# Delta net values and keys put into token order once per head, by VectorE in 32x32 blocks and a trip through DRAM

## The chip, the cores and the metric

The kernel runs on one core of one Trainium2 chip. The metric is the device time of one launch in microseconds (us), lower is better; the median of several launches is given where there are several. TensorE (PE) multiplies matrices, VectorE (DVE), ScalarE (ACT) and GpSimd (POOL) work on tiles, SyncE (SP) mostly starts transfers (DMAs). Each engine takes its instructions strictly in its own order and waits on semaphores for the others.

## The reference

Two layers on a sequence of 1024 tokens of width 1024. Layer 0 has retention (4 heads of 128) and a gated delta net (4 heads of 128), then a feed-forward net; layer 1 has an RG-LRU and a second feed-forward net. The change is in the delta net of layer 0, whose chunkwise form reads:

```python
lmat = where(strict, einsum('bhnid,bhnjd->bhnij', k_beta, kc) * decay, 0)
u, w = triangular_solve(lmat + eye, [vc * bc, k_beta * exp(gc)])
def step(s, (u_n, w_n, a_n, qd_n, kt_n, cd_n)):
    v_new = u_n - w_n @ s
    o = qd_n @ s + a_n @ v_new
    s = s * cd_n + kt_n.T @ v_new
```

with `qkv = silu(causal_dwconv(...))`, `k_tail = kc * exp(g_last - gc)` and `vc` the values by chunk. The kernel takes chunks of 128 tokens, so there are 8 chunks.

## The kernel before

Activations lie as channels x tokens (a head is a tile of 128 channels by 1024 tokens). All large products run as three float32r passes, L313, L314 and L315 in `mm3`: high weights by high data, high by low, low by high. One such instruction of 512 columns is called a *main matmul* below. A projection of 128 output channels (a *unit*) is 48 main matmuls: 8 blocks of the input, 3 passes, and two halves of the tokens. Its weights come in two *quarters*; each is loaded to a `raw` tile (L257, SP), split by ACT into `whi` (L267) and by DVE into `wlo` (L268), in rings of 7 and 6 buffers. The first main matmul of a quarter needs `whi`, the third needs `wlo`.

The program calls `slot()` after each three main matmuls, which steps generators (`lanes`) that carry the small work: the delta net's gates, the substitution, `merge`, `scans` and retention. The tile framework's scheduler then orders the instructions of each engine by its own model of durations; the order is fixed when the program is built, and the chip follows it.

The part of `_mix0` that matters, in order of the units on PE:

- `subst`: 31 steps on DVE invert all 32x32 diagonal blocks of L in tiles `lb` (slots 14 and 15), `tb` (16 and 17) and `tt` (18 and 19); the inverse goes to `t_dram` twice, straight and turned (L1337, L1339).
- `gates2((0, 1))`: units 12 and 13; evacuation by L373, tanh on ACT (L1167), product on DVE (L1168), then a store to `g_dram` (L1716).
- `merge(h, i)` for four heads, i the half of the tokens: blocks come back from `t_dram` (L1353, one set on SP, the turned one on POOL), ACT copies them (L1363, L1364), and PE and ACT take turns: L1369, then L1372 on ACT, L1378 and L1382, then L1385 and L1386 on ACT, L1392, then L1394, L1398. The two halves of a head run together.
- the loop over the value heads: units 24 to 27 (`conv_head`: L373, L1264, three L1266, L1268, L1269), each then stored to `v_dram`.
- `gates2((2,))`: unit 14, a gate like 12 and 13.
- ACT's queue loads the two rotary tables into the halo tiles (L1735, L1736) and DVE multiplies them by the row scale (L1737, L1738).
- `rot_head`: units 0, 4, 1, 5, 2, 6, 3, 7 for retention, evacuated by L1538, L1540 and L1541 on DVE and an addition on POOL.
- `scans`, beside the rotary units: per chunk, `scan_load` brings `v` and `q` from DRAM, `scan_inside` turns the values (L1461, four transposes on PE), scales them (L1462), forms the scores (L1465), turns the keys (L1473) and scales them (L1474, for all chunks but the last); `scan_state` carries the state (L1485, L1491, L1498, L1508, L1509).

Of the kernel before, what the change touches and what calls it, by code (L numbers as in the profile page):

```python
# [13 lines left out]
F32 = mybir.dt.float32  # L14
F32R = mybir.dt.float32r
AF = mybir.ActivationFunctionType
ALU = mybir.AluOpType
AX = mybir.AxisListType

P = 128  # L20
# [3 lines left out]
HALF = 512  # L24
NCH = T // P
NH = 4
# [67 lines left out]
def bc_mid(ap, n):  # L94

    return ap.unsqueeze(1).to_broadcast([ap.shape[0], n, ap.shape[1]])


def bc_last(ap, n):

    return ap.unsqueeze(2).to_broadcast([ap.shape[0], ap.shape[1], n])


class Block:
# [57 lines left out]
    def col(self, name, i):  # L162
        off, n = COLS[name]
        assert i < n
        return self.cols[:, off + i:off + i + 1]
# [978 lines left out]
    def mix0(self, gain):  # L1144
        tc = self.tc
        self.q_dram = tc.dram_tile([NCH, P, HALF], F32, name="q_dram")
        self.ry_dram = tc.dram_tile([4, NCH, P, P], F32, name="ry_dram")
        self.v_dram = tc.dram_tile([NCH, P, HALF], F32, name="v_dram")
        self.gc_dram = tc.dram_tile([NH, NCH, P], F32, name="gc_dram")
        self.l_dram = tc.dram_tile([P, 32, 32], F32, name="l_dram")  # L1150
        self.t_dram = tc.dram_tile([2, P, 32, 32], F32, name="t_dram")
        self.y_dram = tc.dram_tile([8, P, T], F32, name="y_dram")
        self.rv_dram = tc.dram_tile([NCH, P, HALF], F32, name="rv_dram")
        self.g_dram = tc.dram_tile([NH, P, T], F32, name="g_dram")
        self.X = [[(self.slots1(4 * k + n), self.slots1(4 * k + 2 + n)) for n in range(2)] for k in range(KT)]
        with tc.tile_pool(name="l0", bufs=1) as pool:
            gd = self._mix0(pool.tile([P, 24 * HALF], F32, name="l0"))
        self.s2_stack = ExitStack()
        self.open_s2(self.s2_stack)
        self._mix0_out(gain, gd)  # L1160
# [10 lines left out]
    def _mix0(self, room):  # L1171
        tc, nc, I = self.tc, self.nc, self.I
        V, A, G, PE = nc.vector, nc.scalar, nc.gpsimd, nc.tensor
        H = self.H
        ps4 = lambda ps: ps.rearrange("p (h c) -> p h c", h=4)
        hs = lambda h: slice(h * P, (h + 1) * P)
# [9 lines left out]
        slots = lambda i, n=1: room[:, i * HALF:(i + n) * HALF]  # L1186

        def tmp2(name, n=1):
            p = places[name]
            if isinstance(p, tuple):  # L1190
                turn[name] = turn.get(name, 0) + 1
                p = p[turn[name] % 2]
            return slots(p, n)
# [16 lines left out]
        beta, gcc, ngcc, egc, ekt, cen, cdec = (small(n) for n in ("beta", "gcc", "ngcc", "egc", "ekt", "cen", "cdec"))  # L1210
# [49 lines left out]
        def conv_tail(kind, h, buf, dst):  # L1260
            ti = {"q": 0, "k": 4, "v": 8}[kind] + h
            c = self.t()
            w = lambda j: self.col("gdn_conv", 4 * ti + j)
            A.activation(c, buf[:, 1:1 + T], AF.Copy, scale=w(0))  # L1264
            for j in (1, 2, 3):
                V.scalar_tensor_tensor(c, buf[:, 1 + j:1 + j + T], w(j), c, ALU.mult, ALU.add)  # L1266
            th = self.t() if dst is None else dst
            A.activation(th, c, AF.Tanh, scale=0.5)  # L1268
            V.scalar_tensor_tensor(th, th, 1.0, c, ALU.add, ALU.mult)  # L1269
            return th  # L1270

        def conv_head(kind, h, dst):
            unit = conv_unit(kind, h)
            buf = self.next_halo()
            self.project(unit, self.evac_r(buf, 4))
            return conv_tail(kind, h, buf, dst)

        K, L = H[0:4], H[4:8]
        ssk, ssq = small("ssk"), small("ssq")
        rk, sb, ck, cv, irho = (small(n) for n in ("rk", "sb", "ck", "cv", "irho"))  # L1280
# [162 lines left out]
        def scan_load(n):  # L1443
            t = chunk[n]
            t.update({"q": tmp2("qc"), "v": spare["v"][n % 2], "e": spare["e"][n % 2], "kt": spare["kt"][n % 2]})
            nc.sync.dma_start(t["v"], self.v_dram[n])
            nc.sync.dma_start(t["q"], self.q_dram[n])

        def scan_inside(n):
            cs = slice(n * P, (n + 1) * P)  # L1450
            cn = lambda t: hn(t)[:, :, n]
            q, v, gr, e, kt = (chunk[n][i] for i in ("q", "v", "gr", "e", "kt"))
            V.tensor_tensor(ps4(e), ps4(gr), bc_mid(sq["m_attn"], 4), ALU.add)
            for h in range(NH):
                A.activation(e[:, hs(h)], e[:, hs(h)], AF.Exp, bias=col(ngcc, h, n))
            for h in range(NH if n else 0):
                A.activation(gr[:, hs(h)], gr[:, hs(h)], AF.Exp, bias=col(cen, h, n))
            yield
            pv = self.pc()
            for h in range(NH):  # L1460
                PE.transpose(pv[:, hs(h)], v[:, hs(h)], self.ident)  # L1461
            V.tensor_tensor(ps4(v), ps4(pv), bc_last(cn(cv), P), ALU.mult)  # L1462
            p = self.pc()
            for h in range(NH):
                PE.matmul(p[:, hs(h)], K[h][:, cs], q[:, hs(h)], start=True, stop=True)  # L1465
            V.tensor_tensor(e, e, p, ALU.mult)
            if n:
                V.tensor_tensor(q, q, gr, ALU.mult)
            yield
            if n < NCH - 1:  # L1470
                p = self.pc()
                for h in range(NH):
                    PE.transpose(p[:, hs(h)], K[h][:, cs], self.ident)  # L1473
                V.tensor_tensor(ps4(kt), ps4(p), bc_last(cn(ekt), P), ALU.mult)  # L1474
            yield

        def scan_state(n):
# [206 lines left out]
        for h in range(3):  # L1684
            conv_tail("k", h, bufs[h], H[h])
# [17 lines left out]
        for h in range(NH):  # L1703
# [6 lines left out]
            if h % 2:  # L1710
                values(h // 2)

        def gates2(heads):
            for h in heads:
                g = self.gate2(self.unit("mix_in", 12 + h))
                nc.sync.dma_start(self.g_dram[h], g)  # L1716
        scan_row(0)
        gates2((0, 1))
        for h in range(NH):
            v = conv_head("v", h, None)  # L1720
            nc.sync.dma_start(self.v_dram[:, :, hs(h)].rearrange("n p c -> p n c"),
                              v.rearrange("p (n c) -> p n c", n=NCH))
        gates2((2,))
        self.flush()
        S = [tmp2("S0"), tmp2("S1")]
# [16 lines left out]
        for h in range(NH):  # L1742
            q = rot_head(h)
            k = rot_head(4 + h)
            ret += [ret_half(h, i, q, k) for i in range(2)]

        gates2((3,))
        gd = self.gate2(self.unit("mix_in", 28))
        self.flush()
# [118 lines left out]
```

## Time and profile before

| | |
|---|---|
| median of 3 runs | 2149.26 us (2147.45 to 2149.64) |
| profiled execution, whole | 2149.09 us |
| its span in the trace | 2147.3 us |
| granted TensorE clock | 0.999 |
| PE busy in the span | 2131.8 us (99%) |
| DVE busy / ACT busy | 1704.7 (79%) / 1074.1 (50%) |
| `_mix0` from the end of the substitution to the first chunk | about 169 to 263 us |
| the scans | about 263 to 440 us |

A duration in a timeline row is one instruction's from start to end; matmuls overlap, so the pace of PE is read from the distance between starts.

### The profile page before, as it was taken

What the parts mean: (1) busy time and instruction counts of PE and PEld (TensorE: products, weight loads), DVE (VectorE), ACT (ScalarE), POOL (GpSimd) and SP (SyncE); (2) the same over time, 40 slices, a digit from 0 to 9 for tenths busy, and PEclk for the clock granted to TensorE, in tenths of its full rate; (3) what the DMA queues carried; (4) which work ended last, traced back from release to release, by engine and by line L of the source; (5) the groups of instructions that cost most, each with busy time, mean ns of one, the idle gap of its engine ahead of it and who ended that gap; (6) DMA issues with size and microseconds to landing.
All of it is one profiled execution on the core that took longest, in us unless ns stands there. A gap on an engine that the chain in (4) does not pass through costs nothing.

```text
span 2147.3 us, 29614 instructions
## 1 busy us (share of the span) xinstructions
PE 2131.8 (99%) x10652; PEld 1776.5 (83%) x10652; DVE 1704.7 (79%) x2581; ACT 1074.1 (50%) x1732; POOL 96.8 (5%) x114
## 2 busy tenths in 40 slices
PE   9999999999999999999999999999999999999998
PEld 7877888887888888888888888888888888888887
DVE  7995677766999989888766786778999889888645
ACT  6444522234665555555324476755655555554221
POOL 0102022200000000000000000000000000000001
PEclk9999999999999999999999999999999999999999
DMA  5354433543145435438725312252354445375542
GB/s 187 93 168 126 136 94 88 173 146 114 50 163 178 152 141 191 157 113 275 240 99 198 89 50 82 68 157 64 123 181 167 146 154 176 118 267 183 176 169 84
DMA packets 237171, 307.98 MB, mean 143 GB/s; under 512 B 62912, under 2 KB 125920, under 8 KB 237024
## 3 DMA queue, kind: packets, MB, share of 16 engines
q1 hardware_dynamic: 201344, 299.60, 41.8%
q10 hardware_dynamic: 34656, 5.97, 1.5%
q8 instruction: 84, 1.38, 0.3%
q0 software_dynamic: 1024, 0.53, 0.1%
q14 instruction: 63, 0.52, 0.1%
HBM read 215.27 MB, written 90.74 MB: 143 GB/s over the span
## 4 chain that ended last, share of the span: by engine, by line
PE 64%; issue 30%; DVE 3%; DMA 2%; POOL 0%; ACT 0%; SPq 0%; POOLq 0%; DVEq 0%; ACTq 0%
PE ps L313 19%; PE ps L315 19%; PE ps L314 19%; PE pc L313 1%; PE pc L314 1%; PE pc L315 1%; DVE h L973 0%; DVE l L1332 0%; DVE l L1334 0%; PE pc L1491 0%; PE pc L1577 0%; PE pc L1465 0%; PE ps L1509 0%; PE ps L1607 0%; DVE h L1303 0%
## 5 line engine op out<-in xcount | busy, mean ns | idle before, releaser
L313 PE MATMUL ps<-s,whi 128*128 128x512 f32 (+1 forms) x2704 | 1053.6, 390 | 2.5 <-ACT s L586 1.4
L314 PE MATMUL ps<-s,whi 128*128 128x512 f32 (+1 forms) x2704 | 1048.2, 388 | 1.2 <-DVE s L587 0.7
L315 PE MATMUL ps<-s,wlo 128*128 128x512 f32 (+1 forms) x2704 | 1047.5, 388 | 0.0
L267 ACT CAST whi<-raw 128x512 fp32r<-128x512 f32 (+1 forms) x620 | 377.0, 613 | 634.5 <-PE ps L314 499.7
L313 PEld LDWEIGHTS ps<-s,whi 128*128 128x128 f32 x2704 | 507.8, 188 | 108.2 <-ACT s L586 2.3
L314 PEld LDWEIGHTS ps<-s,whi 128*128 128x128 f32 x2704 | 508.0, 188 | 104.5 <-DVE s L900 1.8
L315 PEld LDWEIGHTS ps<-s,wlo 128*128 128x128 f32 x2704 | 507.7, 188 | 104.4 <-DVE wlo L268 0.6
L268 DVE TENSOR_TENSOR wlo<-raw,whi 128x512 fp32r<-128x512 f32 (+1 forms) x620 | 418.0, 680 | 64.0 <-ACT whi L267 55.2
L828 DVE SCALAR_TENSOR_TENSOR t<-halo,cols,t 128x1024 f32<-128x1024 f32 x176 | 221.7, 1281 | 2.1 <-ACT t L826 1.0
L801 DVE TENSOR_TENSOR halo<-ps,kept 128x512 f32<-128x512 f32 (+1 forms) x138 | 92.0, 667 | 76.4 <-PE ps L315 75.6
L811 DVE TENSOR_TENSOR h<-ps,h 128x512 f32<-128x512 f32 x112 | 77.3, 690 | 79.1 <-PE ps L315 79.1
L826 ACT ACTIVATE t<-halo,cols 128x1024 f32<-128x1024 f32 x88 | 109.6, 1247 | 18.0 <-DVE halo L801 9.9
L796 ACT COPY kept<-ps 128x512 f32<-128x512 f32 (+1 forms) x138 | 77.0, 558 | 11.0 <-PE ps L315 9.5
L533 DVE TENSOR_TENSOR h<-ps,h 128x512 f32<-128x512 f32 (+1 forms) x72 | 45.2, 630 | 42.0 <-PE ps L315 41.8
L916 DVE TENSOR_TENSOR t<-t 128x1024 f32<-128x1024 f32 x44 | 53.7, 1221 | 0.0
L911 ACT ACTIVATE t<-t 128x1024 f32<-128x1024 f32 x44 | 46.8, 1063 | 10.0 <-DVE t L828 10.0
L852 ACT CAST t<-t 128x512 fp32r<-128x512 f32 x56 | 34.0, 622 | 34.7 <-DVE t L916 32.7
L401 ACT ACTIVATE t<-h 128x512 f32<-128x512 f32 (+1 forms) x49 | 27.3, 563 | 44.2 <-DVE h L533 44.2
L313 PE MATMUL ps<-s,s 128*128 128x256 f32 (+1 forms) x144 | 46.0, 320 | 0.0
L314 PE MATMUL ps<-s,s 128*128 128x256 f32 (+1 forms) x144 | 45.8, 318 | 0.0
L315 PE MATMUL ps<-s,s 128*128 128x256 f32 (+1 forms) x144 | 45.8, 318 | 0.0
L1266 DVE SCALAR_TENSOR_TENSOR t<-halo,cols,t 128x1024 f32<-128x1024 f32 x33 | 41.9, 1278 | 2.9 <-ACT t L1264 2.6
(337 smaller groups left out, 2113.3 us busy)
## 6 DMA issues: line engine op xcount, KB each, us to landing
raw<-in_ffn_up_dram SPq DMA_DIRECT2D x176, 256.0 KB, 2.7
s<-pf_dram SPq DMA_DIRECT2D x112, 256.0 KB, 5.1
sf_dram<-t SPq DMA_DIRECT2D x72, 256.0 KB, 2.5
raw<-in_ffn_w_dram SPq DMA_DIRECT2D x64, 256.0 KB, 3.0
t<-sf_dram SPq DMA_DIRECT2D x58, 256.0 KB, 4.2
pf_dram<-t SPq DMA_DIRECT2D x56, 256.0 KB, 2.6
pf_dram<-lo SPq DMA_DIRECT2D x56, 256.0 KB, 2.6
raw<-in_mix_in_dram SPq DMA_DIRECT2D x52, 256.0 KB, 3.0
```

What stands on the lines that cost most here:

```text
L267: self.nc.scalar.copy(hi[:, 0:w], raw[:, 0:w])
L268: eng.tensor_tensor(lo[:, 0:w], raw[:, 0:w], f32(hi[:, 0:w]), ALU.subtract)
L313: mm(ps, whi, xhi, start=start, stop=False)
L314: mm(ps, whi, xlo, start=False, stop=False)
L315: mm(ps, wlo, xhi, start=False, stop=stop)
L796: A.copy(kept[o], ps)
L801: V.tensor_tensor(dst(i, j), v(ps), v(kept[k]), ALU.add)
L811: V.tensor_tensor(h(*to[o]), ps.rearrange("p (h c) -> p h c", c=256), h(*to[o]), ALU.add)
L826: A.activation(t, buf[:, 2:2 + T], AF.Identity, scale=w(0), bias=self.col(f"ffn_cb{layer}", tile_i))
L828: V.scalar_tensor_tensor(t, buf[:, 2 + j:2 + j + T], w(j), t, ALU.mult, ALU.add)
L911: A.activation(tg, tg, AF.Silu)
L916: V.tensor_tensor(tg, tg, tv, ALU.mult)
```

## The change

After its convolution each value head is turned by DVE: one instruction transposes every 32x32 block of the 128 x 1024 tile in place of its block grid, and four DMAs then write the blocks to their turned places in DRAM, so that `v_dram[n]` holds chunk n as tokens x channels. Each DMA writes 1024 pieces of 128 bytes. The keys, kept on chip as channels x tokens, are turned in the same way, into the substitution's tiles (slots 14 and 15 for even heads, 16 and 17 for odd ones), and go to a new `k_dram`. The values are turned into the tile `c` that `conv_tail` has finished with. The scans load both and only scale them; the PE transposes L1461 and L1473 and their PSUM tiles are gone.

```diff
@@ mix0
+        self.k_dram = tc.dram_tile([NCH, P, HALF], F32, name="k_dram")
@@ conv_tail
+            free[0] = c
             return th
+        free = [None]
@@ scan_load
             nc.sync.dma_start(t["q"], self.q_dram[n])
+            if n < NCH - 1:
+                nc.sync.dma_start(t["kt"], self.k_dram[n])
@@ scan_inside
-            pv = self.pc()
-            for h in range(NH):
-                PE.transpose(pv[:, hs(h)], v[:, hs(h)], self.ident)
-            V.tensor_tensor(ps4(v), ps4(pv), bc_last(cn(cv), P), ALU.mult)
+            V.tensor_tensor(ps4(v), ps4(v), bc_last(cn(cv), P), ALU.mult)
...
-                p = self.pc()
-                for h in range(NH):
-                    PE.transpose(p[:, hs(h)], K[h][:, cs], self.ident)
-                V.tensor_tensor(ps4(kt), ps4(p), bc_last(cn(ekt), P), ALU.mult)
+                V.tensor_tensor(ps4(kt), ps4(kt), bc_last(cn(ekt), P), ALU.mult)
@@ before the value heads
+        def store_turned(dram, x, h, t):
+            V.transpose(t, x)
+            to = dram.rearrange("n (b i) c -> i (n b) c", i=32)
+            for d in range(4):
+                bs = slice(32 * d, 32 * d + 32)
+                nc.sync.dma_start(to[:, :, h * P + 32 * d:h * P + 32 * d + 32],
+                                  t[bs].rearrange("i (b j) -> i b j", j=32))
@@ the loop over value heads
             v = conv_head("v", h, None)
-            nc.sync.dma_start(self.v_dram[:, :, hs(h)].rearrange("n p c -> p n c"),
-                              v.rearrange("p (n c) -> p n c", n=NCH))
+            store_turned(self.k_dram, K[h], h, slots(14 + 2 * (h % 2), 2))
+            store_turned(self.v_dram, v, h, free[0])
```

The scheduler answers with another order on every engine. Line numbers of the change are larger than those of before by 1 to 8 in this part (L1369 is now L1373, L1378 is L1382, L1382 is L1386, L1392 is L1396, L1398 is L1402, L1363 is L1367, L1167 is L1168, L1168 is L1169, L1736 is L1744, L1738 is L1746). Three places follow.

First, PE at the merge of head 3 (tile `h7`). Before, it stands inside value unit 27, with 12 main matmuls between one step and the next:

```order
L315 MATMUL ps_2324<-s1_96,wlo_1919 128x512
L1369 MATMUL pc_2333<-l0_118,h7_95 32x32 x8
L1369 MATMUL pc_2346<-l0_118,h7_95 32x32 x8
L313 MATMUL ps_2324<-s1_96,whi_1918 128x512
L314 MATMUL ps_2324<-s1_96,whi_1918 128x512
```

Now it stands at the start of rotary unit 0, whose first quarter is `whi_2286` and `wlo_2287`, right behind the last main matmul of gate unit 14 (`ps_2531`), and its steps are 1 to 3 main matmuls apart:

```order
L315 MATMUL ps_2531<-s1_96,wlo_2113 128x512
L313 MATMUL ps_2581<-s1_96,whi_2286 128x512
L314 MATMUL ps_2581<-s1_96,whi_2286 128x512
L1373 MATMUL pc_2361<-l0_119,h7_95 32x32
L315 MATMUL ps_2581<-s1_96,wlo_2287 128x512
L313 MATMUL ps_2581<-s1_96,whi_2286 128x512
L1373 MATMUL pc_2361<-l0_119,h7_95 32x32 x7
L314 MATMUL ps_2581<-s1_96,whi_2286 128x512
L1373 MATMUL pc_2374<-l0_119,h7_95 32x32
L1382 MATMUL pc_2397<-l0_119 32x32 x8
L1386 MATMUL pc_2398<-l0_119 32x32 x8
```

Heads 2 and 3 have thus moved from value units 26 and 27 into gate unit 14 and rotary unit 0. Head 2's first piece now stands 95 main matmuls later than before, and its steps are as close.

Second, ACT's casts of the weights of rotary unit 0. Before, the first (`whi_2431`) stands among the pieces of head 3's merge; the only tanh ahead of it there is that of value head 2 (`t_2252`):

```order
L1364 COPY l0_118<-l0_118 128x512 x2
L1268 ACTIVATE t_2252<-t_2247 128x1024
L1735 DMA halo0_98<-in_rope_dram 128x1024
L1372 COPY l0_118<-pc_2333 32x128 x2
L1372 COPY l0_118<-pc_2346 32x128 x2
L267 CAST whi_2431<-raw_2429 128x512
```

Now it (`whi_2286`) follows the last pieces of head 2's merge, the load of the second rotary table and the tanh of gate unit 14 (`t_2478` is its evacuated result):

```order
L1398 COPY l0_119<-pc_2253 64x256
L1403 COPY h6_94<-l0_119 128x512
L1368 COPY l0_119<-l0_119 128x512 x2
L1744 DMA halo1_99<-in_rope_dram 128x1024
L1168 ACTIVATE t_2557<-t_2478 128x1024
L267 CAST whi_2286<-raw_2284 128x512
```

The cast has moved from within the value heads to behind the end of gate unit 14.

Third, DVE at the same weights. Before, `wlo_2432` and `wlo_2438` of rotary unit 0 are written between the evacuations of value unit 27 (`ps_2268`, `ps_2324`):

```order
L373 TENSOR_TENSOR halo1_99<-ps_2268,R_97 128x512
L1269 SCALAR_TENSOR_TENSOR t_2252<-t_2252,t_2247 128x1024
L268 TENSOR_TENSOR wlo_2432<-raw_2429,whi_2431 128x512
L1737 TENSOR_TENSOR halo0_98<-halo0_98,R_97 128x1024
L1453 TENSOR_TENSOR l0_118<-l0_118 128x512
L373 TENSOR_TENSOR halo1_99<-ps_2324,R_97 128x512
L268 TENSOR_TENSOR wlo_2438<-raw_2435,whi_2437 128x512
```

Now the same two follow the evacuation of the second half of gate unit 14 (`ps_2531`), the product of the second table (`halo1`) and the gate's product:

```order
L373 TENSOR_TENSOR t_2478<-ps_2531,R_97 128x512
L1746 TENSOR_TENSOR halo1_99<-halo1_99,R_97 128x1024
L1169 SCALAR_TENSOR_TENSOR t_2478<-t_2557,t_2478 128x1024
L268 TENSOR_TENSOR wlo_2287<-raw_2284,whi_2286 128x512
L268 TENSOR_TENSOR wlo_2293<-raw_2290,whi_2292 128x512
```

A little later on DVE, the first quarter of rotary unit 4 (`wlo_2469`) follows the evacuation of the second half of rotary unit 0 (`ps_2614`):

```order
L1540 TENSOR_TENSOR l0_119<-ps_2581,halo1_99 64x512
L1541 TENSOR_TENSOR l0_119<-ps_2581,halo1_99 64x512
L1538 TENSOR_TENSOR t_2580<-ps_2614,halo0_98 128x512
L1540 TENSOR_TENSOR l0_119<-ps_2614,halo1_99 64x512
L1541 TENSOR_TENSOR l0_119<-ps_2614,halo1_99 64x512
L268 TENSOR_TENSOR wlo_2469<-raw_2466,whi_2468 128x512
```

Both writes have moved behind work that starts only when the unit just ahead of them on PE has ended. On SP the eight new stores per head stand between the reloads for the merges and the loads of `raw`: between the store of `t_dram` and the last value store there were 12 loads of weights, and there are 3.

## The prediction

> **What bounds the kernel now.** I read the page's totals first, then PE's waits, then the three stretches that the change touches (columns: stretch, its length, busy time and instructions of PE, weight loads, DVE, ACT and POOL, granted clock, share of the DMA engines, GB/s).
>
> ```profile
> span 2147.3 us, 29614 instructions
> PE 2131.8 (99%) x10652; PEld 1776.5 (83%) x10652; DVE 1704.7 (79%) x2581; ACT 1074.1 (50%) x1732; POOL 96.8 (5%) x114
> ```
> ```profile
> PE pc L483 <- POOL rtok L466: 1.7, 2, 1.4
> ...
> PE pc L1369 <- DMA l<-t_dram: 1.0, 2, 0.6
> ```
> ```profile
> 160.00:200.00 40.00, 39.04 (x308) 31.37 (x307) 20.33 (x42) 16.67 (x37) 11.18 (x20) 1.00 0.45 136
> ```
> ```profile
> 200.00:262.00 62.00, 62.00 (x570) 49.57 (x570) 38.94 (x46) 35.15 (x82) 6.63 (x12) 1.00 0.42 123
> ```
> ```profile
> 262.00:440.00 178.00, 178.00 (x1131) 158.43 (x1130) 132.27 (x257) 46.32 (x100) 49.69 (x40) 1.00 0.44 120
> ```
>
> PE is the bound everywhere: in the merges and the scans it is never idle, apart from 1.0 us where head 0's merge waits for its blocks. So an instruction taken from PE is a gain at its full pace, and any wait that PE does not have now is a loss. DVE has 20 us free in the first stretch and 23 in the second. The forecast is therefore a balance of transposes removed against waits created by the new order.
>
> **What is removed.** The pace of PE around one group of key transposes, with the main matmuls that follow:
>
> ```profile
> 265.35 0.39 PE L315 MATMUL ps<-s,wlo 128*128 128x512 f32 x1
> 265.58 0.60 PE L1473 MATMUL pc<-ident,h 128*128 128x128 f32 x4
> 265.94 0.48 PE L313 MATMUL ps<-s,whi 128*128 128x512 f32 x1
> 266.25 0.39 PE L314 MATMUL ps<-s,whi 128*128 128x512 f32 x1
> 266.48 0.40 PE L315 MATMUL ps<-s,wlo 128*128 128x512 f32 x1
> ...
> 269.90 0.39 PE L315 MATMUL ps<-s,wlo 128*128 128x512 f32 x1
> ```
> ```profile
> L1473 PEld LDWEIGHTS pc<-ident,h x28: 138/140/143, 265.4 to 377.2; 128*128 128x128 f32 x28
> L1473 PE MATMUL pc<-ident,h x28: 270/272/273, 265.6 to 377.3; 128*128 128x128 f32 x28
> ```
> ```profile
> 263.02 0.44 PE pc L1461 x4
> ...
> 265.75 0.44 PE pc L1473 x4
> ```
>
> From 266.48 to 269.90 are 15 main matmuls: 0.228 us each. From 265.35 to 266.25 pass 0.90 us in which two main matmuls would take 0.46, so four transposes cost 0.44; the chain's pieces (start, us) say the same of both kinds. The 270 ns of one transpose overlap with the next. There are 8 groups of value and 7 of key transposes: 15 x 0.44 = **6.6 us off PE**.
>
> **What is added on DVE.** Eight transposes of 128x1024. The nearest row has half the width:
>
> ```profile
> L1426 DVE STREAM_TRANSPOSE l<-l 128x512 f32<-128x512 f32 x8 | 5.7, 708 | 0.1
> ```
> ```profile
> L1468 DVE TENSOR_TENSOR l<-l 128x512 f32<-128x512 f32 x4 | 2.7, 682 | 0.0
> ```
>
> So 1.4 us each, 11 in all, within the 43 us that DVE has free; at nothing by themselves. The scaling of values and keys now reads SBUF alone, like L1468 at 0.68 us; from PSUM a product of this size takes 0.69 (L1538, below): nothing.
>
> **What is added in transfers.** 32 stores of 128 KB instead of 4 of 512 KB, in 128-byte pieces, and 7 loads of keys. In the window 150 to 460 us:
>
> ```profile
> q10 hardware_dynamic: 34080, 5.25, 9.3%
> ```
> ```profile
> v_dram<-t SPq DMA_DIRECT2D x4, 512.0 KB, 4.1
> ```
>
> Nearly all packets of q10 are ACT's stores of 128-byte pieces (64 stores of 512). They took 9.3% of 16 engines over 310 us, 461 us over 34080 packets: 13.5 ns each. The 32768 new ones take 28 us of the 16 engines' time over some 80 us in which they are 42 to 45% busy: room. On SP some 35 more issues of about 0.4 us make the loads of `raw` later, but the first one that matters (rotary unit 0) goes out when value head 2 has been stored, some 16 us before PE wants it, and landing takes 3 to 4. Nothing, with the rival below if the pieces are slower. [...] If each piece cost what one of 512 bytes does, the sum would be that of the third rival.
>
> **What the new order costs.** Here lies the price. The durations that the hand-over between PE and ACT takes in a merge, and those of the gate's end:
>
> ```profile
> 217.56 1.10 ACT L1372 COPY l<-pc 32x128 f32<-32x128 f32 x4 [2.61 <-PE pc L1369]
> 218.95 1.06 ACT L1268 ACTIVATE t<-t 128x1024 f32<-128x1024 f32 x1 [0.29 <-DVE t L1266]
> 221.16 0.55 ACT L1385 ACTIVATE l<-pc 32x128 f32<-32x128 f32 x2 [1.15 <-PE pc L1378]
> ...
> 225.28 0.37 ACT L1394 COPY l<-pc 64x256 f32<-64x256 f32 x1 [1.21 <-PE pc L1392]
> 225.55 0.62 ACT L1399 COPY h<-l 128x512 f32<-128x512 f32 x1
> ...
> 226.86 0.62 ACT L1363 COPY l<-l 128x512 f32<-128x512 f32 x1
> ...
> 248.50 0.33 ACTq L1736 DMA_DIRECT2D halo<-in_rope_dram  x1
> ...
> 255.92 1.06 ACT L1167 ACTIVATE t<-t 128x1024 f32<-128x1024 f32 x1
> ```
> ```profile
> 252.79 1.23 DVE L1738 TENSOR_TENSOR halo<-halo,R 128x1024 f32<-128x1024 f32 x1 [1.44 <-DMA halo<-in_rope_dram]
> ...
> 255.14 0.68 DVE L373 TENSOR_TENSOR t<-ps,R 128x512 f32<-128x512 f32 x1
> 255.74 0.68 DVE L268 TENSOR_TENSOR wlo<-raw,whi 128x512 fp32r<-128x512 f32 x1
> 257.01 1.23 DVE L1168 SCALAR_TENSOR_TENSOR t<-t 128x1024 f32<-128x1024 f32 x1 [0.59 <-ACT t L1167]
> 260.34 0.69 DVE L1538 TENSOR_TENSOR t<-ps,halo 128x512 f32<-128x512 f32 x1 [2.10 <-PE ps L315]
> ```
>
> *Head 0's merge.* K of head 1 is turned into the tile that the first `t_dram` store still reads, and DVE waits for it; the gate's product, SP's gate store and behind that SP's reload of the blocks follow.
>
> ```profile
> 168.83 0.33 SPq L1337 DMA_DIRECT2D t_dram<-l  x1
> ```
> ```profile
> 174.05 4.57 POOL L1353 DMA_DIRECT2D l<-t_dram  x8 [52.55 <-DMA t_dram<-l]
> ```
> ```profile
> l<-t_dram SPq DMA_DIRECT2D x32, 16.0 KB, 2.1
> ```
>
> The store lands at 174.05 (what releases POOL). Add 1.4 (turn), 0.7 (L373), 1.1 (tanh), 1.2 (product), three issues of about 0.4, 2.1 to land: 181.7. PE comes there at about 180.2 and waits 1.2 to 1.5 where it waited 1.0: +0.3 (0 to 1.5).
>
> *Merge of head 2.* Its steps stand 1 to 3 main matmuls apart (0.2 to 0.7 us), while ACT needs, for both halves, 1.1 (L1372), 2.2 (L1385 and L1386), 1.2 (L1363), 1.1 for the tanh of value head 3 that stands among them, and 0.4 + 0.6 + 0.4 (L1394, L1399, L1394): 7.0 us, with some six hand-overs of 0.1 to 0.2. PE has about 2.7 us of main matmuls in it and about 3 us of the merge's own. Followed step by step, PE waits about 1.0 before the second half's L1378 and 1.0 behind it: +2.0 (0 to 2.5).
>
> *End of gate unit 14.* The third main matmul of rotary unit 0 needs `wlo_2287`. By way of the tanh: L373 0.7, tanh 1.1, product 1.2, `wlo` 0.7, with starts of hand-overs 3.7 us, less the two main matmuls that can go ahead: 3.3 at least. By way of the table: counted from the last L1382 of head 2, ACT has 1.1 (L1385, L1386), 2.0 (L1394 and L1399 twice) and 1.2 (L1364 twice), with waits 4.6, then starts the load; 4.3 to land (248.50 to 252.79); 1.2 table, 1.2 product, 0.7 `wlo`: 12.0. PE has by then about 21 main matmuls (4.8), 2.1 of the merge, and 1.0 of the waits just counted: 7.9. It waits 12.0 - 7.9, about 4.2 (3.3 to 5.1): I take **+4.2**.
>
> *Merge of head 3.* The same chain without the tanh of a value head, more tightly placed: waits of about 0.4, 0.7 and 0.8, with hand-overs +2.2 (0 to 2.5).
>
> *First quarter of rotary unit 4.* `wlo_2469` follows L1538, L1540 and L1541 of the half just finished: 3 x 0.7 + 0.7 = 2.8, less two main matmuls of 0.46, with a hand-over: **+2.5** (1.9 to 2.6). Later `wlo` stand a unit or more ahead of their use.
>
> *Smaller pieces.* Behind a group of small matmuls the second main matmul starts after 0.31 instead of 0.23 (265.94 to 266.25). I count 72 groups in merges and scans where there were 68, though five that were key transposes alone are gone and already paid: +9 x 0.09 = +0.8 (0.4 to 1.5).
>
> Sum: -6.6 + 0.3 + 2.0 + 4.2 + 2.2 + 2.5 + 0.8 = **+5.4 us**. The profiled execution took 2149.09 (0.17 below the median of 2149.26), so **2154.5 us**. With all lower ends -1.0 (2148.1), with all upper ends +9.1 (2158.2).
>
> **Rivals.** The bound of what a measurement here tells from no change is 0.2%, 4.3 us.
>
> 1. *The waits only make up for the gain* (same). The merges' hand-overs hide and the gate waits for its tanh alone: -6.6 + 0.3 + 3.3 + 2.5 + 0.8 = +0.3, 2149.4. For it: PE hides such hand-overs today at 12 main matmuls. Against: ACT's sum above exceeds PE's work there.
> 2. *A transpose costs PE more than its pace* (faster). If the 270 ns and the weight load's 140 stood one behind the other, 60 x 0.41 = 24.6 us would go: 2136.5. It decides from about 0.27 us each, where 60 of them outweigh 12.0 us of costs by 4.3. Against it stand the starts above.
> 3. *The small pieces hold up SP* (much slower). If a store of 1024 pieces took the 4.1 us of the value store before, one after the other, the 24 ahead of rotary unit 0's weights take 98 us from 174 on, until 272; PE wants these at about 251: some 20 us more, 2174. Against: eight may be under way at once, and 13.5 ns.
> 4. *The clock falls behind the gate's wait* (slower). The granted clock is 1.00 in all rows, but the longest wait of PE in them is 1.4 us. If PE ran at half pace for as long as it had stood still, 4.2 us, it would lose 2.1: 2156.6. The wait is broken by two main matmuls. [...]
>
> **Chances.** Forecast 0.52, rival 1 0.25, rival 2 0.07, rival 3 0.06, rival 4 0.10. The forecast's own range is 2148.1 to 2158.2; a quarter of it (0.13) lies within 0.2%. Slower: 0.39 + 0.06 + 0.10 = 0.55; same: 0.13 + 0.24 = 0.37; faster: 0.07 + 0.01 = 0.08. Leaving out rivals 2 and 3 and the thin ends, the range is 2147.5 to 2160.
>
> **What would show it.** PE's waits get new rows: L315 or L313 on DVE `wlo` and ACT `whi`, about 4 us at the start of rotary unit 0 and 2.5 us at that of unit 4; L1382 and L1402 on ACT, some 4 us in sum; L1373 on a DMA about 1.3. The scans show no new wait, and PE's busy time between them is 6.6 us less. DVE's eight transposes take 1.4 us each. A `whi` or `wlo` that waits for `raw` would speak for rival 3, a clock under 1.00 around 250 us for rival 4. I am wrong if PE passes the end of unit 14 without a gap.

## The result, and the profile after

The changed kernel takes **2168.57 us** (median of 4 runs, 2166.28 to 2172.38) against 2148.78 us before (4 runs): ratio 1.0094 (95% interval 1.0082 to 1.0107), 19.8 us slower. Forecast were 2154.5 us and a range up to 2160: the direction was right, the size was not. The profiled execution took 2169.6 us, 20.5 more than the one before.

The totals, PE's waits (us in all, times, longest) and the three stretches that were shown of before, with the columns that the prediction names:

```profile
span 2167.8 us, 29548 instructions
PE 2141.7 (99%) x10592; PEld 1780.2 (82%) x10592; DVE 1711.9 (79%) x2589; ACT 1072.3 (49%) x1732; POOL 97.9 (5%) x114
```
```profile
PE pc L1491 <- DVE l L1487: 3.0, 1, 3.0
PE ps L315 <- DVE wlo L268: 2.9, 2, 2.5
PE ps L313 <- ACT whi L267: 2.4, 1, 2.4
PE ps L1606 <- DVE l L1600: 2.2, 4, 1.0
...
PE pc L1373 <- DMA l<-t_dram: 1.4, 1, 1.4
```
```profile
160.00:200.00 40.00, 38.60 (x277) 30.28 (x277) 22.60 (x43) 15.29 (x33) 11.14 (x20) 1.00 0.48 121
200.00:262.00 62.00, 59.06 (x515) 45.29 (x515) 39.04 (x40) 27.66 (x59) 6.60 (x12) 0.96 0.44 85
262.00:440.00 178.00, 170.39 (x1037) 148.67 (x1038) 126.01 (x243) 50.37 (x120) 47.45 (x37) 0.94 0.51 140
```

PE is "busy" 99% as before, and yet 20 us are gone. The figure to look at is the granted clock: 1.00 in all three stretches before, now 0.96 and 0.94. A PE at half clock counts as busy (5.00 of 5 us at a clock of 0.50 from 265 to 270 us). Cut finer, the same view shows where:

```profile
255.00:260.00 5.00, 4.05 (x55) 2.42 (x55) 2.40 (x3) 2.10 (x5) 0.00 (x0) 0.67 0.65 104
260.00:265.00 5.00, 5.00 (x66) 3.41 (x61) 0.00 (x0) 3.00 (x11) 0.00 (x0) 0.50 1.31 194
265.00:270.00 5.00, 5.00 (x32) 3.96 (x31) 0.84 (x2) 3.08 (x7) 0.00 (x0) 0.50 1.03 362
...
284.00:288.00 4.00, 4.00 (x16) 3.32 (x15) 3.33 (x6) 1.28 (x4) 0.00 (x0) 0.57 0.10 25
...
344.00:348.00 4.00, 4.00 (x14) 3.42 (x14) 0.79 (x2) 1.72 (x3) 0.00 (x0) 0.50 0.12 19
350.00:355.00 5.00, 5.00 (x25) 4.13 (x24) 1.30 (x3) 0.00 (x0) 1.30 (x1) 1.00 0.20 52
```

The trace's clock records have three stretches at half: 17.07 us, 3.41 us and 6.83 us. Half of their sum, 13.65 us, is what the clock withheld; it cost at most that, for waits of PE that would have come in these stretches anyway are hidden in it. Each stretch starts in the last microsecond of a wait of PE or just behind it (at 256.75, 284.06 and 342.08 us; the waits end at 256.86, 282.68 and 342.99). The first wait is at the start of rotary unit 0 (timeline, all engines):

```profile
252.74 0.39 PE L315 MATMUL ps<-s,wlo 128*128 128x512 f32 x1
253.16 0.69 DVE L373 TENSOR_TENSOR t<-ps,R 128x512 f32<-128x512 f32 x1 [2.58 <-PE ps L315]
253.89 1.06 ACT L1168 ACTIVATE t<-t 128x1024 f32<-128x1024 f32 x1 [3.73 <-DVE t L373]
254.85 1.13 ACT L267 CAST whi<-raw 128x512 fp32r<-128x512 f32 x2
255.50 0.50 PE L313 MATMUL ps<-s,whi 128*128 128x512 f32 x1 [2.38 <-ACT whi L267]
256.12 1.28 DVE L268 TENSOR_TENSOR wlo<-raw,whi 128x512 fp32r<-128x512 f32 x2
256.86 0.79 PE L315 MATMUL ps<-s,wlo 128*128 128x512 f32 x1 [0.45 <-DVE wlo L268]
```

This is the predicted chain, but PE stops in it two main matmuls sooner than forecast, at the first one, which needs `whi`. ACT had stood still for 3.73 us, with the raw weights there, but the tanh of gate unit 14 came first in its order, and that waited for DVE's L373, and that for PE. PE stood still for 2.38 and 0.45 us. The second wait is the predicted one of rotary unit 4, 2.50 us against 2.5 forecast:

```profile
279.80 0.39 PE L314 MATMUL ps<-s,whi 128*128 128x512 f32 x1
282.68 0.50 PE L315 MATMUL ps<-s,wlo 128*128 128x512 f32 x1 [2.50 <-DVE wlo L268]
```

The third was not foreseen. SP issues the load of a chunk's keys at 331.62; it lands 6.4 us later, at 338.0. DVE's order has the scaling of these keys (L1474) ahead of L1487, for which PE waits:

```profile
331.62 0.44 SPq L1453 DMA_DIRECT2D kept<-k_dram  x1
...
338.03 0.69 DVE L1474 TENSOR_TENSOR kept<-kept,l 128x512 f32<-128x512 f32 x1 [3.11 <-DMA kept<-k_dram]
...
342.58 1.12 DVE L1487 SCALAR_TENSOR_TENSOR l<-pc,l 128x128 f32<-128x128 f32 x4
```
```profile
342.99 2.08 PE L1491 MATMUL pc<-l,h 128*128 128x128 f32 x8 [3.03 <-DVE l L1487]
```

The added work itself cost what was forecast: DVE's transposes take 1.24 us each, and stores of 128 KB in 128-byte pieces land after 3.0 and 3.4 us (mean of a transpose; then issue to landing).

```profile
L1714 DVE STREAM_TRANSPOSE t<-t 128x1024 f32<-128x1024 f32 x4 | 5.0, 1246 | 0.1
```
```profile
k_dram<-l SPq DMA_DIRECT2D x16, 128.0 KB, 3.0
v_dram<-t SPq DMA_DIRECT2D x16, 128.0 KB, 3.4
```

### The profile page after: what moved, and what is told of

It reads as the page before. It is cut to its first block, busy times and chain, and to the rows that moved or that the text cites. A ratio compares the mean times of both kernels' runs of the same rounds, so it can differ in the third digit from the quotient of the medians.

```text
span 2167.8 us, 29548 instructions
## 1 busy us (share of the span) xinstructions
PE 2141.7 (99%) x10592; PEld 1780.2 (82%) x10592; DVE 1711.9 (79%) x2589; ACT 1072.3 (49%) x1732; POOL 97.9 (5%) x114
## 3 DMA queue, kind: packets, MB, share of 16 engines
q0 software_dynamic: 1024, 0.53, 0.1%
## 4 chain that ended last, share of the span: by engine, by line
PE 64%; issue 29%; DVE 3%; DMA 2%; POOL 1%; ACT 0%; SPq 0%; POOLq 0%; DVEq 0%; ACTq 0%
PE ps L313 19%; PE ps L315 19%; PE ps L314 19%; PE pc L313 1%; PE pc L314 1%; PE pc L315 1%; PE ps L1557 0%; PE ps L1559 0%; PE ps L1558 0%; PE pc L1491 0%; PE pc L1468 0%; DVE h L973 0%; DMA kept<-k_dram 0%; PE pc L483 0%; PE ps L1606 0%
```

## The experiments

Theory C: waits of PE over some 2.3 us let the clock fall to half, and that made most of the loss. Rivals: P, the 128-byte pieces hold up the transfers; M, the crowded merges cost it; O, the waits alone. Each group of runs had its own runs of the kernel before (medians 2148.2 to 2149.0). The last column leaves out the end of the program, where every trace, that of before too, has 7 to 11 us at half. The trace is of one execution of a kernel, the median of all.

| run | median us | ratio to before, 95% interval | half clock in the trace, us |
|---|---|---|---|
| changed kernel | 2168.57 | 1.0094 (1.0082 to 1.0107) | 17.07, 3.41, 6.83 |
| merge blocks by POOL | 2164.97 | 1.0080 (1.0067 to 1.0094) | 6.83, 3.41, 3.41 |
| three queues | 2173.08 | 1.0118 (1.0104 to 1.0131) | 3.41, 6.83, 6.83, 6.83 |
| whole rows | 2153.76 | 1.0019 (1.0010 to 1.0028) | 3.41, 3.41 |
| scale later | 2168.50 | 1.0093 (1.0079 to 1.0107) | 17.07, 3.41, 6.83 |
| whole rows, late | 2153.28 | 1.0023 (1.0012 to 1.0033) | 10.24, 3.41 |
| values alone | 2145.74 | 0.9990 (0.9981 to 0.9998) | none |
| keys by ACT | 2155.85 | 1.0034 (1.0022 to 1.0046) | 6.83, 3.41 |
| scale behind state | 2164.70 | 1.0073 (1.0061 to 1.0085) | 13.65, 3.41 |
| weights ahead | 2166.79 | 1.0082 (1.0069 to 1.0095) | 17.07, 3.41 |
| both orders | 2160.62 | 1.0051 (1.0037 to 1.0064) | none in the trace |
| keys by ACT, behind | 2153.80 | 1.0023 (1.0013 to 1.0033) | 6.83 |
| transposes twice | 2154.11 | 1.0024 (1.0015 to 1.0034) | none |
| values unturned | 2145.06 | 0.9980 (0.9971 to 0.9989) | none |

**Gaps by themselves.** A kernel of its own: `gap(ps, cols)` is a chain of DVE instructions that writes the weights of the next burst, `small` is the turn-taking with ACT.

```python
    for cols in ((), (P,), (512,), ..., (512, 512, 512, 512, 512)):
        for _ in range(3):
            gap(ps, cols)
            ps = burst(80)
    for main in (1, 2, 4):
        for _ in range(3):
            gap(ps, (512, 512, 512)); burst(4); small(6, main)
            ps = burst(80)
```

> Not the reference: only bursts of 80 main matmuls (128x512), kept apart by DVE work that the next burst waits for, three times each of nine lengths, from some 0.5 to 4.5 us of PE standing still; then nine times a gap of some 2.5 us behind which stand six small groups of 32x32 matmuls that take turns with ACT, with 1, 2 or 4 main matmuls between. Theory C (the clock gate made most of the loss): from some length on, of about 2.3 to 3 us, the matmuls behind a gap start 0.43 us apart instead of 0.23, for about 5 us where only main matmuls follow, and for more than 10 us where the small groups follow; gaps under 1.5 us do nothing. Theory O (the waits alone): 0.23 us behind every gap. The rule as my fourth rival had it (half pace for as long as the gap): 1 us behind a gap of 1, 4 behind one of 4.

The clock by windows, behind a gap of 2.2 us, behind two of 2.65 (one that was followed by half clock and one that was not), and behind one with small groups:

```profile
264.00:272.00 8.00, 7.15 (x32) 5.95 (x33) 0.67 (x2) 0.00 (x0) 0.00 (x0) 1.00 0.00 1
...
327.00:335.00 8.00, 7.89 (x28) 6.36 (x29) 0.00 (x0) 0.00 (x0) 0.00 (x0) 0.79 0.00 0
349.00:357.00 8.00, 7.23 (x32) 6.02 (x33) 0.59 (x2) 0.00 (x0) 0.00 (x0) 1.00 0.01 2
...
703.00:713.00 10.00, 8.96 (x60) 6.30 (x61) 1.09 (x3) 1.12 (x3) 0.00 (x0) 0.54 0.00 0
713.00:723.00 10.00, 10.00 (x64) 7.08 (x63) 0.00 (x0) 1.12 (x3) 0.00 (x0) 0.50 0.01 2
```
```profile
327.11 6.19 PE L1873 MATMUL ps<-xr,w 128*128 128x512 f32 x19 [2.65 <-DVE w L1880]
```

PE's idle time (the bracket) and how often half clock followed: up to 2.19 us none of 15; 2.65 us one of 3; 2.92 us two of 3; 3.64 us two of 3; 4.37 us three of 3. Behind them, with main matmuls only, it lasted 3.41 us, once 6.83. With small groups behind a gap of 2.6 to 2.7 us all nine fell, eight of them for 17.07 or 20.48 us. (In PE's order 3, 3 and 4 main matmuls stand between these groups where the source asks for 1, 2 and 4.)

Which gap trips the clock is not chance. All 17 stretches at half start on one grid of 3.41 us: those at 328.31, 393.17 and 437.54 us, for example, are 19 and 13 steps apart. Cut into the windows of that grid, the record shows how much of a gap lies in each (idle time is the length less PE's busy time):

```profile
304.42:307.83 3.41, 1.79 (x8) 1.51 (x9) 1.41 (x3) 0.00 (x0) 0.00 (x0) 1.00 0.00 0
324.90:328.31 3.41, 1.20 (x5) 1.05 (x6) 1.96 (x4) 0.00 (x0) 0.00 (x0) 1.00 0.00 0
...
458.02:461.43 3.41, 1.39 (x6) 1.20 (x7) 1.77 (x4) 0.00 (x0) 0.00 (x0) 1.00 0.00 0
...
481.91:485.33 3.42, 1.63 (x7) 1.40 (x8) 1.58 (x3) 0.00 (x0) 0.00 (x0) 1.00 0.00 0
```

These four windows hold 1.62, 2.21, 2.02 and 1.79 us of idle time. The clock fell at the end of the second and third, and not behind the other two, although the last is half of a gap of 3.64 us: an edge of the grid cuts that gap in two. Over the 27 gaps with main matmuls alone, all eight windows with 2.02 us of idle time or more were followed by half clock, and none with 1.90 or less. The three gaps of 2.19 us had at most 1.62 us in one window, so they do not show that 2.2 us is harmless. In the changed kernel the clock fell behind windows with 2.51, 2.04 and 2.13 us of idle time. Counted by main matmuls at their pace of 0.228 us it holds in all 16 traces: among the windows at full clock that held main matmuls alone, the clock fell behind all 21 with fewer than 5.9 of them, and behind none with 5.98 or more. With small groups in the window less idle time was enough (1.10 to 1.75 us in four of the nine trials).

So theory C holds, with two amendments: the fall goes with the idle time inside one window of the grid (2.02 us or more with main matmuls alone), not with the length of the gap alone, and small groups behind the gap went with a longer half clock (17.07 or 20.48 us in eight of nine trials, against 3.41 with main matmuls only, once 6.83). My rule (half pace for as long as the gap) is wrong: the length comes in steps of 3.41 us, five or six of them in those eight trials, and hangs on what follows.

**The merges back in their old places.** Both block sets on POOL's queue:

```diff
-                    (nc.sync if q else nc.gpsimd).dma_start(
+                    nc.gpsimd.dma_start(
```

> The changed kernel with one edit: both sets of a merge's blocks are loaded by POOL's queue. PE's order then has all four merges where they stood before (666, 726, 786, 846 main matmuls from the start of the units), while the weights of rotary units 0 and 4 are written as late as in the changed kernel. Theory C: PE still stands still for 2.5 to 3 us at both units and in a scan, but no merge follows the first gap, so the clock is back after some 5 us instead of 17: 8.4 us lost to the clock at unit 0 become about 2.5, and 2 to 3 of hand-overs go: 2160 (2156 to 2163). Theory M (the crowded merges are the loss): 2149 to 2152. Theory P (32768 pieces of 128 bytes hold up the DMA engines): 2168 as before.

Measured 2164.97, above theory C's range of 2156 to 2163, below P's 2168 and far from M's 2152: none of the three came out. The trace shows why C's sum missed. At unit 0 the same gap stands (2.38 us), and the half clock behind it is 3.41 us long instead of 17.07, as C has it:

```profile
260.00:265.00 5.00, 2.25 (x9) 1.23 (x7) 2.55 (x4) 2.95 (x5) 0.00 (x0) 1.00 0.69 151
265.00:270.00 5.00, 4.98 (x15) 3.95 (x16) 0.57 (x1) 0.99 (x3) 0.00 (x0) 0.66 0.95 308
```

But the edit made a new gap: PE waits 3.07 us for the blocks of head 0, which now all come by POOL's queue, and 6.83 us of half clock follow from 183.9 us on.

**Three queues.** Key stores by POOL (in halves), SP's merge blocks by ACT:

```diff
-                    (nc.sync if q else nc.gpsimd).dma_start(
+                    (nc.scalar if q else nc.gpsimd).dma_start(
...
-                nc.sync.dma_start(to[:, :, h * P + 32 * d:h * P + 32 * d + 32],
+                for n in (0, 4): nc.gpsimd.dma_start(to[:, 4 * n:4 * n + 16, ...
```

> The changed kernel with its transfers on three queues: key stores on POOL's (each in two halves), value stores on SP's as they were, the merge blocks that SP loaded on ACT's. PE's order has merges and scans where they stood in the kernel before, and the weights of units 0 and 4 are written a unit ahead. The bytes and pieces are the same as in the changed kernel. Theory C: no gap at units 0 and 4, so 2.8 + 8.4 and 2.5 + 2.3 us come back: 2152; 2146 if the scan's wait for keys (3.0 and 2.9 of clock) goes too. Theory P: 2165 or more.

Slower still, 2173.08. That lies beyond P's 2165, but it is no verdict on P, for the edit held up the merges. On POOL's queue one key store comes only about 2.5 us after the other, and the merge's blocks stand behind them; PE then waits 5.36 us, and 4.72 us at a later one:

```profile
207.06 0.66 POOL L1720 DMA_DIRECT2D k_dram<-l  x1 [2.49 <-issue]
209.51 0.65 POOL L1720 DMA_DIRECT2D k_dram<-l  x1 [1.80 <-issue]
212.01 0.66 POOL L1720 DMA_DIRECT2D k_dram<-l  x1 [1.85 <-issue]
```
```profile
228.54 0.75 PE L1382 MATMUL pc<-l 32*32 32x32 f32 x11 [5.36 <-ACT l L1376]
```

**Whole rows.** One store of 512-byte pieces per head; the scheduler then keeps the order of before:

```diff
-            to = dram.rearrange("n (b i) c -> i (n b) c", i=32)
-            for d in range(4): ...
+            nc.sync.dma_start(dram[:, :, hs(h)].rearrange("n p c -> p n c"),
+                              t.rearrange("p (n c) -> p n c", n=NCH))
```

> The changed kernel with one store of 512-byte pieces in the place of four of 128: the blocks stay at their old places, so the scans get values and keys in a wrong arrangement; the number of bytes, DVE transposes, key loads and the missing PE transposes are as in the changed kernel, and the order of merges and weights is that of before. It prices what the change takes from PE: 15 groups at 0.44 us, 2142.5, or up to 2149 if a scan waits for its keys. If a transpose cost PE 0.41 us (my second rival): 2125.

2153.76, above both forecasts: without the reordering 15 of the 20 us are gone, yet even so nothing is gained. (The pieces changed too, so this run does not tell the order from P; the run with both orders, below, does.) The keys again: DVE stands 3.33 us for a load of keys, PE then waits 2.18 us for DVE, and 3.41 us of half clock follow in the scans. As many follow at head 0's merge, behind two waits of only 1.06 and 1.41 us.

```profile
301.68 0.69 DVE L1474 TENSOR_TENSOR l<-l 128x512 f32<-128x512 f32 x1 [3.33 <-DMA l<-k_dram]
```
```profile
303.22 0.49 PE L1606 MATMUL ps<-l 128*128 128x128 f32 x2 [2.18 <-DVE l L1600]
```

**Scaling the keys later**, as a line moved in the program (in the changed kernel and in the whole-rows one):

```diff
@@ scan_inside
-            if n < NCH - 1:
-                V.tensor_tensor(ps4(kt), ps4(kt), bc_last(cn(ekt), P), ALU.mult)
@@ scan_state, at its start
+            if n < NCH - 1:
+                V.tensor_tensor(ps4(kt), ps4(kt), bc_last(cn(ekt), P), ALU.mult)
```

> The changed kernel with one line moved: the keys of a chunk are scaled (L1474) where the state needs them, at the start of scan_state, instead of at the end of scan_inside. PE's order and the weights stay as in the changed kernel. Theory K (DVE stood 3.1 us at that line for a load that took 6.4 us to land, and held up the row that PE waited 3.0 us for; the clock then gave half for 6.8 us): the wait of 3.0 and 0.4, 3.4 of clock and perhaps the 2.2 of L1606 go: 2160 to 2162, with the two gaps at units 0 and 4 as they were. Rival (the keys come too late wherever they are scaled): the wait turns up on L1498, 2167 or more.

> The run with whole rows (values and keys in a wrong arrangement, the order of merges and weights as in the kernel before) with two edits: keys scaled where the state needs them, and all heads' keys turned in slots 14 and 15, which no store of the substitution reads. Theory: of its 2153.8 the waits for keys (3.7 at L1606, 1.8 at L1491, 1.7 of clock) and most of head 0's merge (1.5, 1.7 of clock) go: 2144 to 2146; that is the price of the transposes, 3 to 5 us for 15 groups. If 0.44 a group is right in full: 2142.5. If DVE's added turning costs PE something by itself: 2148 or more.

Both missed, 2168.50 and 2153.28: the scheduler left the scaling of the keys (L1474, now L1481) in its old place in DVE's order, so in the first PE waited 2.9 us for L1487 as before. Nothing follows on the keys. In the second, head 0's merge waited 2.6 us for its blocks and cost 10.24 us of half clock; why the shared slots made that worse was not followed up.

**Scaling behind the state**, now with an edge of order:

```diff
-                    V.scalar_tensor_tensor(v[:, hs(h)], p[:, hs(h)], ...)
+                    last = V.scalar_tensor_tensor(v[:, hs(h)], p[:, hs(h)], ...)
...
+                with tc.issue_after(last.ins):
+                    V.tensor_tensor(ps4(kt), ps4(kt), bc_last(cn(ekt), P), ALU.mult)
```

> The changed kernel with an edge of order on DVE: the keys of a chunk are scaled behind the state's L1487 of the same chunk (the run that only moved the line kept its place in DVE's order, right behind the row that waits). Nothing else moves. Theory K: PE's wait of 2.9 to 3.0 us at L1491, its 3.4 us of half clock, and part of the 2.2 at L1606 go: 2160 to 2163. Rival (the keys land too late for the state too): 2167 or more, with a new wait at L1498.

2164.70, 3.9 us less, and still above theory K's 2163. The wait of 3.0 us and the third stretch of half clock are gone; in this trace the first stretch is shorter too (13.65 us). But L1606's row (now L1610) still waits 2.5:

```profile
PE ps L1610 <- DVE l L1604: 2.5, 4, 1.4
...
PE pc L1495 <- DVE l L1485: 1.2, 2, 0.9
```

**Weights ahead, and both orders.** Edges put the casts of unit 0 ahead of gate unit 14's tanh, and its low parts and unit 4's ahead of evacuations:

```diff
+        with self.behind(nxt, 0):      # ACT: after unit nxt's whi
+            self.nc.scalar.activation(th, g, AF.Tanh, scale=0.5)
...
+            with self.behind(nxt, 1) if n else ExitStack():   # DVE: after its wlo
+                evac(n, sl, ps)
```

> The changed kernel with edges of order on ACT and DVE alone: the casts of rotary unit 0's weights ahead of gate unit 14's tanh, their low parts ahead of the evacuation of its second half and of the second rope product, and those of rotary unit 4 ahead of the evacuation of unit 0's second half. All transfers, queues and PE's order (heads 2 and 3 crowded into gate unit 14 and rotary unit 0) stay. Theory C: both gaps go (2.4 + 0.4 and 2.5), and with them 8.5 and 1.7 of clock; head 3's hand-overs, so far hidden in the half clock, show 2 to 3: 2154 to 2157. Rival M (the crowded merge itself lets the clock fall): the half clock stays near 258 us, 2162 or more.

> The changed kernel with the edges of both runs before: weights of units 0 and 4 ahead, keys scaled behind the state. Bytes, pieces, queues and PE's order as in the changed kernel. Theory C and K together: no half clock at all; what is left is the 6.6 of transposes against the crowded merges (some 4 to 5 us of hand-overs) and 2 to 3 of waits in the scans: 2147 to 2151. Theory P (pieces): 2160 or more.

The first missed: 2166.79, with half clock from 256.9 us on, which was the sign that rival M named. The trace shows a gap there all the same. Both predicted gaps are gone, but a little later PE waits 2.07 us for the blocks of head 3's merge, which SP loads from 254.0 on, and the clock falls. The weights' gap had hidden that one.

```profile
256.43 0.21 PE L1389 MATMUL pc<-l,h 32*32 32x32 f32 x2 [2.07 <-DMA l<-t_dram]
```
```profile
255.00:260.00 5.00, 3.57 (x23) 2.11 (x24) 1.99 (x2) 2.48 (x5) 0.00 (x0) 0.69 0.47 76
260.00:265.00 5.00, 5.00 (x90) 3.29 (x89) 0.00 (x0) 2.66 (x10) 0.00 (x0) 0.50 1.40 177
```

With both edits the median, 2160.62, missed as well and lies beyond P's 2160. But the executions differ, and they show the clock's share best of all. In the one that was traced the wait at the blocks is 1.8 us and the clock stays up:

```profile
240.00:275.00 35.00, 32.51 (x346) 24.10 (x345) 17.90 (x24) 18.24 (x45) 6.28 (x7) 1.00 0.73 175
```

One kernel, six executions, granted clock and span in us: 0.999, 2151.4; 0.997, 2154.5; 0.995, 2157.5; 0.994, 2160.1; 0.993, 2161.1; 0.993, 2162.4. Span times the clock that is missing against 0.999 is 0, 4, 9, 11, 13 and 13 us; without it the spans are 2148 to 2151. So the spread of 11 us goes with the clock. Which gap fell in the other five was not traced. The profiled execution, with no half clock, took 2153.20, with the pieces, bytes and queues of the changed kernel: P cannot account for the 20 us. M keeps about 4.6 us: from value unit 26 to the end of rotary unit 0 this trace loses 3.75 us against that of before (by the start of the same main matmul), though two groups of transposes (0.9) are gone there; 2.0 of it is the wait for head 3's blocks.

**Other ways to hand the work out.** Values alone (keys transposed by PE as before, head 3's blocks by POOL); the whole change with the key stores on ACT, without and with the edge:

```diff
-                    (nc.sync if q else nc.gpsimd).dma_start(
+                    (nc.sync if q and h < 3 else nc.gpsimd).dma_start(
...
-            store_turned(self.k_dram, K[h], h, slots(14 + 2 * (h % 2), 2))
+            store_turned(self.k_dram, K[h], h, slots((14, 20)[h % 2], 2), "k")   # stores by nc.scalar
```

> The values alone go by DVE and DRAM, as in the changed kernel; the keys are transposed by PE as before. Head 3's merge loads both sets of blocks on POOL's queue, so PE's order has all merges where they stood before, and the weights come early. 16 stores of 1024 pieces of 128 bytes. Theory C: no gap above 2 us, 8 groups of 0.44 gone: 2145 to 2147. Theory P (the small pieces cost time): 2152 or more.

> The whole change, with the bytes and pieces as they are: the keys' stores are issued by ACT, values' by SP; the keys are turned in slots 14 and 15 or 20 and 21; they are scaled where the state needs them; head 3's merge loads both sets of blocks on POOL. PE's order has merges and scans as before, weights early. Theory C: no gap, no half clock: 2143 to 2147. Theory P: 2160 or more. If the 16 issues on ACT (0.6 us each) hold up its part of the merges: 2150 to 2155.

> The run with the keys' stores on ACT (order of merges as before), with the keys scaled behind the state by an edge as well. Theory K: the 9.5 us that it lost in one place of the scans (a wait of 2.8 and 5.1 of clock among it) go: 2145 to 2147, as fast as the values alone or faster by the 3 us of the key transposes. Rival: the wait turns up on L1498, 2152 or more.

The values alone take 2145.74, 2.5 us faster than before: 16 stores of 128-byte pieces, no long wait, no half clock. It is the one complete version that beats both kernels, if by little (0.9981 to 0.9998). The two runs with all keys missed their forecasts. The key stores on ACT cost the merges nothing, but gaps of 2.84 and 2.17 us stay in the scans, with 6.83 and 3.41 us of half clock behind them (2155.85); with the edge one gap of 2.87 us trips the clock, for 6.83 us (2153.80). DVE is late there in a stretch in which ten loads of weights (6.9 us to land) share SP's queue with the loads of the chunks; what decides it was not settled.

**The price of a group.**

```diff
@@ transposes twice: scan_inside, values and keys alike
-            for h in range(NH):
+            for h in [*range(NH), *range(NH)]:
@@ values unturned: scan_inside
-            pv = self.pc()
-            for h in range(NH): PE.transpose(pv[:, hs(h)], v[:, hs(h)], self.ident)
-            V.tensor_tensor(ps4(v), ps4(pv), bc_last(cn(cv), P), ALU.mult)
+            V.tensor_tensor(ps4(v), ps4(v), bc_last(cn(cv), P), ALU.mult)
```

> The kernel before, with every group of value and key transposes done twice into the same place (15 groups, 60 more transposes), the rest of PE's order nearly unchanged. The prediction's pace (0.44 us a group): 6.6 more, 2155.6. If the gain never showed because PE has slack around the groups (the hand-overs of the scans would wait anyway): 2 to 3 more, 2151 to 2152.

> The kernel before without its 8 groups of value transposes and nothing put in their place: the values are scaled where they lie, channels by tokens, so the scans get them in a wrong arrangement. At 0.44 a group: 3.5 less, 2145.5. If other waits of the scans take up part, as the 2.2 that the run with the values alone gained in the scans hints: 2146.5 to 2147.

15 more groups cost 5.3 us (ratio interval: 3.2 to 7.3), 8 fewer give 3.7 (2.4 to 6.2). Compared by the start of the same main matmul in both traces, the first three units of the scans, with two groups each, are 0.86 to 0.88 us longer with doubled groups, and 0.43 to 0.45 shorter without the values' one. That is the 0.44 a group of the prediction. Over the whole of the scans it is 6.2 us for the 15 groups, and only 2.4 for the 8. So the gain was there, and other things took it.

## Why the prediction was wrong

The two traces were compared by the start of the same main matmul. The changed kernel loses 22.0 us between head 0's merge and the end of the scans; 1.6 come back behind them, near 488 us, where the trace of before waits longer for ACT and DVE, so 20.4 are left by the last one. The merges' hand-overs are what is left of the 15.4 us lost from value unit 26 to rotary unit 4, less 10.2 of clock, the waits of 2.8 and 2.5, and with 1.8 back for four groups:

| step | forecast | measured |
|---|---|---|
| transposes off PE | -6.6 | -6.6 by the price of a group (-6.2 over the whole scans) |
| head 0's merge | +0.3 | about +1.0 |
| merges of heads 2 and 3, hand-overs | +4.2 | about +1.6 visible, part of it under the half clock (4.6 in the run with both orders) |
| end of gate unit 14 | +4.2 | +2.8 (2.38 and 0.45) |
| first quarter of rotary unit 4 | +2.5 | +2.5 |
| new waits in the scans | none | +5.2 (3.0 and 0.4 at L1491, 1.6 at L1606, 0.2 at L1485) |
| half clock | 0 (2.1 in the fourth rival) | +13.65 at most |
| small blocks and the rest | +0.8 | +0.2, what is left of 20.4 (-1.6 behind the scans in it) |

- *Right*: the price of a group; PE's waits at head 0's merge and at units 0 and 4, and on whom (the rows L1382 and L1402 on ACT, some 4 us, did not appear); DVE's and the stores' cost as nothing, where 1.4 us a transpose was forecast and 1.24 came; the second rival (transposes dearer) as unlikely. The gate's end came out at the shorter of its two ways, by the tanh: the rope table had landed by then.
- *The step that failed* is the fourth rival's term, "half pace for as long as it had stood still, 4.2 us, it would lose 2.1", and its chance of 0.10. It was priced for one gap; there were three. Behind the first stood the merge of head 3, and with its 32x32 groups following the clock stayed at half for 17.07 us. The rival named the fall and the place. No run shows its term, half pace for as long as the wait; in its place the runs showed half clock in steps of 3.41 us, behind waits of 2.38 and 0.45, of 2.50 and of 3.03 us in the changed kernel. The kernel before has no wait of PE above 1.4 us, so the rate and the length were the author's estimate, and 0.10 was too little for the one rival that spoke against the forecast's own waits.
- *The term that was left out* is "7 loads of keys", counted only as bytes. They are read by DVE, whose order puts the scaling of one chunk's keys so close behind their load that DVE stood still for 3.11 of the 6.4 us that it took to land; why the scheduler chose that place is not shown. "The scans show no new wait" was wrong by 5.2 us and by the third stretch of half clock.
- Without the clock the sum nearly held, but by luck in part: the four runs' spans less the clock lost against before (0.9986) are about 2153.5, 2154.1, 2153.7 and 2154.5, with the 1.8 us around a span some 2155.7, against 2154.5. Read so, the merges were priced about 3 too high and the scans 5 too low. But half clock hides hand-overs: in the run with both orders, where nothing hides them, the crowded merges cost 4.6, near the 4.2 forecast.
- The third rival's 2174 lies near the result for the wrong reason: no cast waited for `raw` at unit 0; ACT idled beside weights that had landed.

## What to carry to other kernels

Where PE is the bound, a new wait is not priced by its length alone. In the gap kernel, with main matmuls on both sides, 2.02 us or more of it inside one 3.41 us window was followed by 3.41 us at half clock (once 6.83), half of which is lost; where small matmuls followed, by 17.07 or 20.48 us in eight of nine trials. Beside small matmuls shorter waits did it in the runs (2.07 us in one, 1.06 and 1.41 us close together in another). Of the nine waits of 2.65 to 3.64 us in the gap kernel with main matmuls alone five were followed by half clock and four were not, by where they fell in the grid. So, by these figures, look first for waits above 1 us beside small matmuls and above 2 us elsewhere, read the granted clock in narrow windows (PE's busy share hides a half clock: 99% before and after), and check the program's order, for each load that a busy engine consumes, how far the consumer stands behind the issue. Moving a line in the source need not move it in the order; an edge does.

## What was not expected of the hardware

- The granted clock has two rates here, 1.00 and 0.50, and each stretch at half starts on one grid of 3.41 us within its trace and is a multiple of it, in all runs (but for the one at a program's end).
- Small groups by themselves did not lower the clock (1.00 in the merges of the kernel before, from 160 to 262 us), but where they followed a gap of 2.6 to 2.7 us it stayed at half for 17.07 or 20.48 us in eight of nine trials.
- On POOL's queue, stores of 512 pieces of 128 bytes follow each other at about 2.5 us in the run with three queues, though the engine is busy for only 0.66 us of each; on SP's queue, in the changed kernel, stores twice as large go out within about 0.6 us (0.55 and 0.63 us in the median, keys and values).
